# A two-layer Griffin and pooling trunk: another source for four weight units, another order inside a head, another order of seven products, another end

## The chip, the cores and the metric

The kernel runs on one core of one Trainium2 chip. A core has a matrix engine (TensorE, PE), a vector engine (VectorE, DVE), a scalar engine (ScalarE, ACT), a general engine (GpSimd, POOL) and a sync engine (SyncE, SP) that here only starts transfers. The metric is the device time of one call in microseconds (us); the kernel before has a median of 1735.13 us over 3 runs (1734.38 to 1735.78).

## The reference

One sequence of 1024 tokens, width 1024, two layers. Each layer adds a gated token mixer and then a gated squared-ReLU MLP; layer 0 mixes with a Griffin recurrent block, layer 1 with a pooling mixer. Cut to what matters here:

```python
def recurrent_mixer(h, w_y, b_y, w_in, b_in, conv_w, conv_b, w_a, b_a, w_x, b_x, lam, w_out, b_out):
    gate_branch = jax.nn.gelu(h @ w_y + b_y)
    xr = causal_depthwise_conv(h @ w_in + b_in, conv_w, conv_b)      # width 4
    gate_r = sigmoid(block_diag_linear(xr, w_a, b_a))                # 4 heads of 256 channels
    gate_i = sigmoid(block_diag_linear(xr, w_x, b_x))
    log_a = 8 * gate_r * log_sigmoid(lam); a = exp(log_a)
    u = sqrt(-expm1(2 * log_a)) * (gate_i * xr)
    xr = scan(a, u)                                                  # h_t = a_t h_(t-1) + u_t
    return (xr * gate_branch) @ w_out + b_out

for i in range(2):
    x = x + gt_m * mixer_i(modulate(rms_norm(x, g_mix), sh_m, sc_m))
    h = modulate(rms_norm(x, g_ffn), sh_f, sc_f)
    x = x + gt_f * (relu(h @ w1) ** 2 @ w2)                          # 1024 -> 4096 -> 1024
return rms_norm(x, g_final)
```

## The kernel before

Channels lie on the 128 partitions, in 8 blocks of 128; the tokens lie along the free axis, in two halves of 512 (`H`). Half 0 is a tile named `...a` (`xa`, `xca`), half 1 one named `...b`. Every float32 product is made of three matmuls (`mm3`, lines 188 to 190): the operand is split into a high part and a remainder, and high by high, high by remainder and remainder by high are added in one PSUM tile. A projection of one output block over 1024 inputs takes 24 matmuls of 128x512; `acc_mm()` gives the PSUM tiles, six of them in turn, so a product waits until the tile of the sixth product before it has been read.

A weight unit of 128x1024 is loaded and split in two halves of 512 columns. ACT casts the high part (line 180) and DVE subtracts to get the remainder (line 181). In the form `"dma"` (`neg_part`) ACT casts (163) and writes the negated high part (164), and a transfer that POOL starts (165) adds the weight from memory to it; no DVE work is in it.

The stages, in order of time: 0 to 66 us the conditioning, the first norm and the first projections; 66 to 120 us the second half of the input projections `w_in` with the convolutions (line 452 copies a product to `xr`, 459 makes the first of the four taps on ACT, 466 the three others on DVE, or 463 on ACT and 464 on POOL for two of the 16 blocks); up to about 250 us the four heads; then `w_out`, and from 355 us the MLP of layer 0, the pooling mixer and the MLP of layer 1, and the end.

In a head (line 583 on), each half goes through `gates` (the input's split at 534, sigmoids 544, exp and tanh 551 and 552, DVE's product 557, square root 560, scan 564) and then through two `gelu_block`s (572): per half 24 matmuls of gates and 48 of gelu. Sigmoid, exp and tanh, square root and gelu each need their own activation table, so ACT loads four tables per half.

In an MLP round `f2_fast` (line 783 on) makes the second product with seven block products in place of eight, four times (`r` = 0 to 3), six matmuls to a product. What becomes of a product: 1 is copied by ACT and scaled, and POOL adds it to `xb`; 5 and 3 are added by DVE to `xa` (800; 5 twice); 6 is summed by DVE with the copy of 1 (830), scaled by ACT (804) and added by POOL to `xa` (809); 7 is summed on top of that (834), scaled, and added by POOL to both halves; 2 and 4 are added by DVE to `xb`. 3 and 6 go to the same block of `xa`. Their order before is 1, 5, 6, 3, 7, 2, 4.

Each engine works through its own queue in order. The program is written once; a scheduler orders each engine's instructions, with `tc.issue_after` as a bound, and the one DVE instruction that carries the conditioning vector's products (`mb`, line 207) is spread over the heads and rounds as its transfers land ("drip").

At the end the last 256 tokens of half 1 are normed: line 1067 scales blocks 0 and 1 ahead of time into `two`, 1070 copies the broadcast factor for POOL, 1072 multiplies on POOL, 1035 makes blocks 2 to 7 on DVE, and SP starts the four stores (1073, 1037).

## Time and profile before

| what | value |
|---|---|
| median of 3 runs | 1735.13 us (1734.38 to 1735.78) |
| the profiled execution | 1736.2 us, its span 1734.4 us |
| PE busy | 1690.3 us, 97% of the span, 7482 matmuls |
| DVE, ACT, POOL busy | 75%, 58%, 31% |
| mean granted clock of TensorE | 0.994 |

The span runs from the first to the last instruction that the profiler saw; 1.8 us of the execution lie around it. A share of busy time is a mean over stages: here PE is busy nearly always, and the few places where it is not are found by asking what it waited for, and in which stretch.

### The profile page before, as it was taken

The numbers are of one execution on the slowest core, as the hardware profiler recorded it, in microseconds if no ns is written. First come the engines' busy times: TensorE is split into PE (matmuls) and PEld (weight loads), VectorE is DVE, ScalarE is ACT, GpSimd is POOL, SyncE is SP. The second block draws the span as 40 slices with busy tenths as digits, with TensorE's granted clock in tenths as the row PEclk, the third lists the DMA queues.
The fourth block names the chain that finished last, engine by engine and source line by source line (L and its number), as shares of the span: only waits on it lengthen the run. The fifth ranks groups of instructions, "written<-read, shape, count | busy, mean of one in ns | idle before, by whom it ended". The sixth has DMA issues, their size and how long they took to land.

```text
span 1734.4 us, 21031 instructions
## 1 busy us (share of the span) xinstructions
PE 1690.3 (97%) x7482; PEld 1388.3 (80%) x7482; DVE 1308.3 (75%) x2066; ACT 1003.0 (58%) x1717; POOL 538.9 (31%) x471
## 2 busy tenths in 40 slices
PE   6999999999999999999999999999999999999997
PEld 4778778887878888888888888888888888888887
DVE  7896977499898989897973898548586867677646
ACT  5868886565445454545457787756555555555532
POOL 1142343104141405051416233324241516051503
PEclk9999999999999999999999999999999999999998
DMA  9432425552423333342319898872323324150502
GB/s 356 138 104 92 146 86 163 116 153 78 134 82 113 101 94 113 94 124 83 121 43 203 194 195 186 185 163 69 89 79 68 100 52 111 43 121 25 134 1 97
DMA packets 70952, 201.50 MB, mean 116 GB/s; under 512 B 7616, under 2 KB 10048, under 8 KB 70848
## 3 DMA queue, kind: packets, MB, share of 16 engines
q1 hardware_dynamic: 47376, 157.43, 28.2%
q0 software_dynamic: 23472, 42.74, 15.0%
q8 instruction: 58, 0.95, 0.2%
q14 instruction: 46, 0.38, 0.1%
HBM read 195.94 MB, written 4.19 MB: 115 GB/s over the span
## 4 chain that ended last, share of the span: by engine, by line
PE 65%; DVE 19%; issue 6%; ACT 4%; POOL 3%; DMA 2%; DVEq 0%; SPq 0%; ACTq 0%; POOLq 0%
PE mm L188 21%; PE mm L189 21%; PE mm L190 21%; DVE xa L800 2%; POOL xa L809 2%; DVE xb L800 2%; DVE mb L207 1%; DMA mb<-in_wmod 1%; DVE w_a_s L181 1%; DVE raw_w L755 1%; ACT c L804 1%; DVE w_a_a L181 1%; DVE xcb L466 1%; DVE xca L466 1%; PE mm L427 1%
## 5 line engine op out<-in xcount | busy, mean ns | idle before, releaser
L188 PE MATMUL mm<-hh,w_w 128*128 128x512 f32 x1024 | 399.1, 390 | 0.0
L189 PE MATMUL mm<-hl,w_w 128*128 128x512 f32 x1024 | 398.6, 389 | 0.0
L190 PE MATMUL mm<-hh,w_w 128*128 128x512 f32 x1024 | 398.5, 389 | 0.0
L809 POOL TENSOR_TENSOR xb<-xb,c 128x512 f32<-128x512 f32 x104 | 151.2, 1454 | 567.0 <-ACT c L804 566.5
L188 PEld LDWEIGHTS mm<-hh,w_w 128*128 128x128 f32 x1024 | 192.2, 188 | 41.3 <-DVE xa L800 1.6
L190 PEld LDWEIGHTS mm<-hh,w_w 128*128 128x128 f32 x1024 | 192.2, 188 | 39.9
L189 PEld LDWEIGHTS mm<-hl,w_w 128*128 128x128 f32 x1024 | 192.2, 188 | 39.9
L809 POOL TENSOR_TENSOR xa<-xa,c 128x512 f32<-128x512 f32 x104 | 157.0, 1510 | 132.3 <-ACT c L804 132.3
L804 ACT ACTIVATE c<-c,mod 128x512 f32<-128x512 f32 x104 | 75.3, 724 | 175.9 <-DVE c L830 113.5
L165 POOL DMA_DIRECT2D w_w<-in_w x136 | 121.6, 930 | 176.9 <-ACT w_w L164 135.8
L650 ACT ACTIVATE relu<-mm 128x512 f32<-128x512 f32 x128 | 76.2, 595 | 143.0 <-PE mm L190 143.0
L800 DVE SCALAR_TENSOR_TENSOR xa<-mm,mod,xa 128x512 f32<-128x512 f32 x156 | 113.3, 744 | 41.6 <-POOL xa L809 41.6
L207 DVE SCALAR_TENSOR_TENSOR mb<-mb,cond 128x1024 f32<-128x1024 f32 x80 | 114.5, 1434 | 33.2 <-DMA mb<-in_wmod 33.0
L163 ACT CAST w_w<-raw_w 128x512 fp32r<-128x512 f32 x136 | 83.0, 611 | 29.1 <-PE mm L190 29.0
L800 DVE SCALAR_TENSOR_TENSOR xb<-mm,mod,xb 128x512 f32<-128x512 f32 x104 | 77.2, 742 | 19.8 <-POOL xb L809 19.0
L164 ACT ACTIVATE w_w<-w_w 128x512 fp32r<-128x512 f32 x136 | 85.7, 631 | 3.6
L188 PE MATMUL mm<-u,w_a_a 128*128 128x512 f32 x200 | 79.2, 396 | 4.0 <-DVE xa L800 2.3
L640 DVE TENSOR_TENSOR u<-usq,u 128x512 fp32r<-128x512 f32 x102 | 70.3, 689 | 16.1 <-ACT u L639 15.8
L188 PE MATMUL mm<-u,w_w 128*128 128x512 f32 (+1 forms) x224 | 81.0, 362 | 0.0
L189 PE MATMUL mm<-u,w_w 128*128 128x512 f32 (+1 forms) x224 | 80.6, 360 | 0.1
L190 PE MATMUL mm<-u,w_w 128*128 128x512 f32 (+1 forms) x224 | 80.4, 359 | 0.0
L189 PE MATMUL mm<-u,w_a_a 128*128 128x512 f32 x200 | 78.0, 390 | 0.0
(330 smaller groups left out, 4026.1 us busy)
## 6 DMA issues: line engine op xcount, KB each, us to landing
raw_w<-in_w SPq DMA_DIRECT2D x148, 512.0 KB, 4.2
mb<-in_wmod SPq DMA_DIRECT2D x80, 512.0 KB, 3.8
w_w<-in_w POOLq DMA_DIRECT2D x136, 256.0 KB, 5.6
mw<-in_wmod SPq DMA_DIRECT2D x16, 512.0 KB, 9.8
raw_in<-in_w_in SPq DMA_DIRECT2D x8, 512.0 KB, 6.0
raw_y<-in_w_y SPq DMA_DIRECT2D x8, 512.0 KB, 3.7
raw_o<-in_w_out SPq DMA_DIRECT2D x8, 512.0 KB, 4.6
outT<-o SPq DMA_DIRECT2D x11, 256.0 KB, 2.9
```

The source lines that it names most:

```text
L163: S.copy(w[:, 0, 0:n], raw)
L164: S.activation(w[:, 1, 0:n], w[:, 0, 0:n].bitcast(F32), AF.Identity, scale=-1.0)
L165: nc.gpsimd.dma_start(w[:, 1, 0:n], src, accum_op=ALU.add)
L188: PE.matmul(out=ps, lhsT=wh, rhs=rh, start=first, stop=False)
L189: PE.matmul(out=ps, lhsT=wh, rhs=rl, start=False, stop=False)
L190: PE.matmul(out=ps, lhsT=w[:, 1, c:c + P], rhs=rh, start=False, stop=last)
L207: V.scalar_tensor_tensor(raw, raw, 1.0, cond, op0=ALU.mult, op1=ALU.mult, accum_out=m[:, e:e + 1])
L640: eng.tensor_sub(u[n][:, 1, jj, :], src, u[n][:, 0, jj, :].bitcast(F32))
L650: S.activation(r, ps, AF.Relu)
L800: V.scalar_tensor_tensor(xb, ps, g[:, r + 4 * row:r + 4 * row + 1], xb, op0=ALU.mult, op1=ALU.add)
L804: S.activation(t, src, AF.Identity, scale=g[:, r + 4 * row:r + 4 * row + 1])
L809: G.tensor_add(xb, xb, t)
```

## The change

It has four parts.

1. `w_in` units 2, 3, 4 and 5 take the form `"dma"`. Units 2 and 3 are asked for right behind the interleaved product of units 6 and 7, ahead of the convolutions of half 0; 4 and 5 inside the loop, two blocks ahead.
2. `gates` is cut in `split_x`, `sigmoids` and `states`, and `gelu_block` in `gelu_blocks` and `gated`. A head now runs gates of half 0, gelu of half 0, gelu of half 1, gates of half 1; the four gelu activations stand behind the square roots of half 0, in one run. The input split of the gates and the gate weights of the next head are issued a round ahead. `w_out` unit 0 is split on DVE, ahead of the last gates; unit 1 to 3 as before on POOL.
3. The default order of the products of `f2_fast` is 1, 5, 3, 6, 7, 2, 4.
4. At the end `two` is scaled earlier, the output blocks share one tile `olast`, DVE starts with block 2, SP stores blocks 2 to 4 and 0 to 1, and ACT's queue stores 5 to 7.

```diff
@@ -485,6 +485,7 @@
     for k in range(NB):
         for m in (6, 7):
             mm3(ps2[m - 6], uin[m], k * P, hh[1][:, k, :], hl[1][:, k, :], k == 0, k == NB - 1)
+    uin.update({m: split_unit(w_in[m], f"in{m}", "dma") for m in (2, 3)})
     for e in last:
         behind.enter_context(tc.issue_after(e.ins))
     for m in range(3, NB):
@@ -492,8 +493,8 @@
     for m in (6, 7):
         conv(m, conv_input(m, ps2[m - 6], 1), 1)
     for m in range(6):
-        if 0 < m < 5:
-            uin[m + 1] = split_unit(w_in[m + 1], f"in{m + 1}")
+        if m in (1, 2):
+            uin[m + 3] = split_unit(w_in[m + 3], f"in{m + 3}", "dma")
         conv(m, conv_input(m, proj(uin[m], hh[1], hl[1]), 1), 1)
 
 
@@ -526,13 +527,17 @@
 
     behind.close()
 
-    def gates(hd, unit, h):
+    def split_x(hd, h):
 
         xchl = slot("xchl", (2, 2, H), F32R)
         xch, xcl = xchl[:, 0, :, :], xchl[:, 1, :, :]
         src = xc[h][:, 2 * hd:2 * hd + 2, :]
         S.copy(xch, src)
         V.tensor_sub(xcl, src, xch.bitcast(F32))
+        return xch, xcl
+
+    def sigmoids(hd, unit, h, xch, xcl):
+
         rs, gs = [], []
         for mi in range(2):
             b = 2 * hd + mi
@@ -543,6 +548,10 @@
                 t = tmp("gate")
                 S.activation(t, ps, AF.Sigmoid, bias=vcol("ba" if g == 0 else "bx", b))
                 (rs if g == 0 else gs).append(t)
+        return rs, gs
+
+    def states(hd, h, rs, gs):
+
         aa = []
         for mi in range(2):
             b = 2 * hd + mi
@@ -557,7 +566,7 @@
             V.scalar_tensor_tensor(rs[mi], e, 1.0, rs[mi], op0=ALU.add, op1=ALU.mult)
         for mi in range(2):
             b = 2 * hd + mi
-            S.activation(rs[mi], rs[mi], AF.Sqrt)
+            root = S.activation(rs[mi], rs[mi], AF.Sqrt)
             hs = xc[h][:, b, :]
             G.tensor_mul(gs[mi], gs[mi], hs)
             V.tensor_mul(gs[mi], gs[mi], rs[mi])
@@ -565,12 +574,19 @@
                                  op0=ALU.mult, op1=ALU.add)
             if h == 0:
                 V.tensor_copy(carry[:, b:b + 1], hs[:, H - 1:H])
-
-    def gelu_block(m, unit, h):
-        ps = proj(unit, hh[h], hl[h])
-        g = tmp("gelu")
-        S.activation(g, ps, AF.Gelu_apprx_tanh, bias=vcol("by", m))
-        V.tensor_mul(xc[h][:, m, :], xc[h][:, m, :], g)
+        return root
+
+    def gelu_blocks(hd, units, h, g, root):
+        for mi in range(2):
+            ps = proj(units[mi], hh[h], hl[h])
+
+            with tc.issue_after(root.ins):
+                S.activation(g[:, 2 * h + mi, :], ps, AF.Gelu_apprx_tanh, bias=vcol("by", 2 * hd + mi))
+
+    def gated(hd, h, g):
+        for mi in range(2):
+            y = xc[h][:, 2 * hd + mi, :]
+            V.tensor_mul(y, y, g[:, 2 * h + mi, :])
 
     yh, yl = [None, None], [None, None]
 
@@ -580,17 +596,32 @@
             S.copy(yh[h][:, k, :], xc[h][:, k, :])
             V.tensor_sub(yl[h][:, k, :], xc[h][:, k, :], yh[h][:, k, :].bitcast(F32))
 
+
+
+    wo = []
+    ug, xs = split_unit(w_g[0], "g0"), [split_x(0, 0), split_x(0, 1)]
     for hd in range(4):
         rate[0] = hd
-        ug = split_unit(w_g[hd], f"g{hd}")
         uy = [split_unit(w_y[m], f"y{m}") for m in (2 * hd, 2 * hd + 1)]
-        for h in range(2):
-            gates(hd, ug, h)
-            if (hd, h) == (3, 1):
-                split_y(0)
-            for mi in range(2):
-                gelu_block(2 * hd + mi, uy[mi], h)
-    wo = [split_unit(w_out[m], f"o{m}", G, 0) for m in range(4)]
+        first = sigmoids(hd, ug, 0, *xs[0])
+        if hd < 3:
+            xs[0] = split_x(hd + 1, 0)
+        root = states(hd, 0, *first)
+        g = slot("gelu")
+        gelu_blocks(hd, uy, 0, g, root)
+        gated(hd, 0, g)
+        gelu_blocks(hd, uy, 1, g, root)
+        if hd < 3:
+            next_ug = split_unit(w_g[hd + 1], f"g{hd + 1}")
+        else:
+            wo.append(split_unit(w_out[0], "o0", None, 0))
+            split_y(0)
+        second = sigmoids(hd, ug, 1, *xs[1])
+        if hd < 3:
+            ug, xs[1] = next_ug, split_x(hd + 1, 1)
+        states(hd, 1, *second)
+        gated(hd, 1, g)
+    wo += [split_unit(w_out[m], f"o{m}", G, 0) for m in range(1, 4)]
     split_y(1)
 
     af = [None, None]
@@ -780,7 +811,7 @@
         w = neg_part(raw, w2[i, c, r, :, 256:768], "a12_a22")
         return {2: (w, 0, (1, 0)), 4: (w, 256, "t4")}
 
-    def f2_fast(i, c, ahead, products=(1, 5, 6, 3, 7, 2, 4), side=iter(())):
+    def f2_fast(i, c, ahead, products=(1, 5, 3, 6, 7, 2, 4), side=iter(())):
 
 
 
@@ -1056,22 +1087,37 @@
                 G.tensor_mul(o[:, k, 0:n1], o[:, k, 0:n1], bc)
             nc.sync.dma_start(osrc[:, k0:k0 + 4, H:H + n1], o[:, k0:k0 + 4, 0:n1])
         yield
+        for k in range(2):
+            S.activation(two[:, k, :], x[1][:, k, n1:H], AF.Identity, scale=vcol("gfin", k))
+        yield
 
     n1 = 256
+    two = tmp("two").rearrange("p (k t) -> p k t", k=2)
     sa = last_chunk(0, 0, H, "VVVVVVVV")
     sb = last_chunk(1, 0, n1, "VVVVVVVV", once(lambda: final_norm(rstd_bcast(sa), 0, 0, H)))
     sc = last_chunk(1, n1, H - n1, "VVVVVVXX", mid_norm())
-
-    two = tmp("two").rearrange("p (k t) -> p k t", k=2)
-    for k in range(2):
-        S.activation(two[:, k, :], x[1][:, k, n1:H], AF.Identity, scale=vcol("gfin", k))
+    o = slot("olast", (NB, H - n1))
     last_bc = rstd_bcast(sc)
     bc_two = tmp("bc_two", H - n1)
+
+    def last_o(k):
+        V.scalar_tensor_tensor(o[:, k, :], x[1][:, k, n1:H], vcol("gfin", k), last_bc, op0=ALU.mult, op1=ALU.mult)
+
+    def store(eng, k0, k1):
+        eng.dma_start(osrc[:, k0:k1, H + n1:2 * H], o[:, k0:k1, :])
+
+
+    last_o(2)
     S.copy(bc_two, last_bc)
     for k in range(2):
-        G.tensor_mul(two[:, k, :], two[:, k, :], bc_two)
-    nc.sync.dma_start(osrc[:, 0:2, H + n1:2 * H], two)
-    final_norm(last_bc, 1, n1, H - n1, 2)
+        G.tensor_mul(o[:, k, :], two[:, k, :], bc_two)
+    for k in (3, 4):
+        last_o(k)
+    store(nc.sync, 2, 5)
+    store(nc.sync, 0, 2)
+    for k in (5, 6, 7):
+        last_o(k)
+    store(nc.scalar, 5, 8)
 
 
 def _layout(inputs):

```

Where the instructions stand now. First POOL's queue at the input projections; `w_in2` and its like are transfers, `xca` and `xcb` the adds of taps (half 0 and half 1). Before:

```order
L165 DMA w_in0_0_595<-in_w_in 128x512
L165 DMA w_in0_512_599<-in_w_in 128x512
L165 DMA w_in1_0_605<-in_w_in 128x512
L165 DMA w_in1_512_609<-in_w_in 128x512
L464 TENSOR_TENSOR xca_1_470<-xca_1_470,tap_724 128x512
L464 TENSOR_TENSOR xca_1_470<-xca_1_470,tap_727 128x512
L464 TENSOR_TENSOR xca_1_470<-xca_1_470,tap_730 128x512
L464 TENSOR_TENSOR xcb_1_472<-xcb_1_472,tap_748 128x512
L464 TENSOR_TENSOR xcb_1_472<-xcb_1_472,tap_751 128x512
L464 TENSOR_TENSOR xcb_1_472<-xcb_1_472,tap_754 128x512
L562 TENSOR_TENSOR gate_1051<-gate_1051,xca_0_469 128x512
```

After the change:

```order
L165 DMA w_in1_0_605<-in_w_in 128x512
L165 DMA w_in1_512_609<-in_w_in 128x512
L165 DMA w_in2_0_713<-in_w_in 128x512
L165 DMA w_in2_512_717<-in_w_in 128x512
L165 DMA w_in3_0_723<-in_w_in 128x512
L165 DMA w_in3_512_727<-in_w_in 128x512
L464 TENSOR_TENSOR xca_1_470<-xca_1_470,tap_744 128x512
L464 TENSOR_TENSOR xca_1_470<-xca_1_470,tap_747 128x512
L464 TENSOR_TENSOR xca_1_470<-xca_1_470,tap_750 128x512
L165 DMA w_in4_0_811<-in_w_in 128x512
L165 DMA w_in4_512_815<-in_w_in 128x512
L165 DMA w_in5_0_853<-in_w_in 128x512
```

Four transfers stand ahead of the six adds, three between their two groups and one behind them. On PE the three units 2, 3 and 4 were begun in turn with two matmuls each before a remainder was first used; now each unit's 24 matmuls stand together:

```order
L188 MATMUL mm_837<-hh1_0_613,w_in2_0_791 128x512
L189 MATMUL mm_837<-hl1_0_615,w_in2_0_791 128x512
L188 MATMUL mm_877<-hh1_0_613,w_in3_0_831 128x512
L189 MATMUL mm_877<-hl1_0_615,w_in3_0_831 128x512
L188 MATMUL mm_917<-hh1_0_613,w_in4_0_871 128x512
L189 MATMUL mm_917<-hl1_0_615,w_in4_0_871 128x512
L190 MATMUL mm_837<-hh1_0_613,w_in2_0_791 128x512
L188 MATMUL mm_837<-hh1_0_613,w_in2_0_791 128x512
```

```order
L188 MATMUL mm_861<-hh1_0_613,w_in2_0_713 128x512
L189 MATMUL mm_861<-hl1_0_615,w_in2_0_713 128x512
L190 MATMUL mm_861<-hh1_0_613,w_in2_0_713 128x512
L188 MATMUL mm_861<-hh1_0_613,w_in2_0_713 128x512
L189 MATMUL mm_861<-hl1_0_615,w_in2_0_713 128x512
L190 MATMUL mm_861<-hh1_0_613,w_in2_0_713 128x512
L188 MATMUL mm_861<-hh1_0_613,w_in2_0_713 128x512
L189 MATMUL mm_861<-hl1_0_615,w_in2_0_713 128x512
```

So PE reads the remainder of unit 2 (line 190) at its third matmul there, where it stood at the seventh.

ACT in one of the heads (lines 534, 544, 560, 572 before; 535, 549, 569, 584 now). Before, behind the tanh of half 0:

```order
L552 ACTIVATE gate_1602<-gate_1602,ncoef_1005 128x512
L534 CAST xchl_1976<-xcb_1_472 128x1024
L560 ACT_TABLE_LOAD
L560 ACTIVATE gate_1584<-gate_1584 128x512
L560 ACTIVATE gate_1602<-gate_1602 128x512
L572 ACT_TABLE_LOAD
L572 ACTIVATE gelu_1660<-mm_1635,vec_79 128x512
L572 ACTIVATE gelu_1688<-mm_1663,vec_79 128x512
L544 ACT_TABLE_LOAD
L544 ACTIVATE gate_1701<-mm_1694,vec_79 128x512
L544 ACTIVATE gate_1710<-mm_1703,vec_79 128x512
```

After the change, from the table of the square roots of the same half on:

```order
L569 ACT_TABLE_LOAD
L569 ACTIVATE gate_1581<-gate_1581 128x512
L569 ACTIVATE gate_1599<-gate_1599 128x512
L584 ACT_TABLE_LOAD
L584 ACTIVATE gelu_1635<-mm_1636,vec_79 128x512
L584 ACTIVATE gelu_1635<-mm_1662,vec_79 128x512
L584 ACTIVATE gelu_1635<-mm_1690,vec_79 128x512
L180 CAST w_y6_0_1830<-raw_y6_1819 128x512
L180 CAST w_y6_512_1833<-raw_y6_1819 128x512
L180 CAST w_y7_0_1847<-raw_y7_1836 128x512
L584 ACTIVATE gelu_1635<-mm_1716,vec_79 128x512
L180 CAST w_y7_512_1850<-raw_y7_1836 128x512
```

The run of sigmoids that stood behind two gelus now stands behind four; a head has seven table loads where it had eight. The weight casts between are those of `w_y`.

DVE in round 2 of layer 1, behind the last weight split for `r` = 3 (830 and 834 before are 861 and 865 now). Before:

```order
L181 TENSOR_TENSOR w_s_10787<-raw_w_1_2_3_10772,w_s_10787 128x256
L800 SCALAR_TENSOR_TENSOR xa_81<-mm,mod_5_6526,xa_81 128x512
L800 SCALAR_TENSOR_TENSOR xa_82<-mm,mod_5_6526,xa_82 128x512
L830 TENSOR_TENSOR c_10797<-mm,c_10797 128x512
L800 SCALAR_TENSOR_TENSOR xa_81<-mm,mod_5_6526,xa_81 128x512
L834 TENSOR_TENSOR c_10797<-mm,c_10797 128x512
L800 SCALAR_TENSOR_TENSOR xb_83<-mm,mod_5_6526,xb_83 128x512
L800 SCALAR_TENSOR_TENSOR xb_84<-mm,mod_5_6526,xb_84 128x512
L800 SCALAR_TENSOR_TENSOR xa_81<-mm,mod_5_6526,xa_81 128x512
```

After the change:

```order
L181 TENSOR_TENSOR w_s_10783<-raw_w_1_2_3_10768,w_s_10783 128x256
L831 SCALAR_TENSOR_TENSOR xa_81<-mm,mod_5_6439,xa_81 128x512
L831 SCALAR_TENSOR_TENSOR xa_82<-mm,mod_5_6439,xa_82 128x512
L831 SCALAR_TENSOR_TENSOR xa_81<-mm,mod_5_6439,xa_81 128x512
L861 TENSOR_TENSOR c_10793<-mm,c_10793 128x512
L865 TENSOR_TENSOR c_10793<-mm,c_10793 128x512
L831 SCALAR_TENSOR_TENSOR xb_83<-mm,mod_5_6439,xb_83 128x512
L831 SCALAR_TENSOR_TENSOR xb_84<-mm,mod_5_6439,xb_84 128x512
```

The third addition to `xa` (product 3) stood behind the sum `c` of product 6; now it stands directly behind the two of product 5, and the two sums follow each other.


## Rows read from the trace of the kernel before

**Rows 1.** TensorE's waits: what it waited for, us in total, times, longest.

```profile
PE mm L188 <- DVE xa L800: 6.6, 8, 1.6
PE mm L188 <- ACT gelu L572: 5.3, 4, 2.2
...
PE mm L190 <- DVE w_in L181: 3.3, 1, 3.3
```

**Rows 2.** Stretches: length, busy time of PE, PEld, DVE, ACT, POOL, then PEclk.

```profile
66.00:120.00 54.00, 50.73 (x211) 41.34 (x210) 52.72 (x89) 40.55 (x65) 23.30 (x10) 0.94 0.34 89
120.00:250.00 130.00, 124.74 (x533) 101.63 (x532) 103.99 (x145) 107.44 (x144) 43.46 (x29) 0.97 0.37 118
415.00:525.00 110.00, 105.39 (x460) 85.70 (x460) 95.79 (x150) 49.84 (x89) 38.88 (x25) 1.00 0.35 112
525.00:900.00 375.00, 374.11 (x1643) 307.37 (x1642) 320.93 (x510) 183.25 (x324) 105.98 (x67) 1.00 0.32 98
1200.00:1640.00 440.00, 437.12 (x1917) 358.76 (x1916) 305.81 (x453) 240.01 (x419) 159.78 (x138) 1.00 0.34 82
```

**Rows 3.** The same view over two stretches at the lower granted clock.

```profile
97.51:104.33 6.82, 6.00 (x14) 4.75 (x15) 6.82 (x8) 3.03 (x4) 5.22 (x4) 0.50 0.21 64
179.42:182.82 3.40, 3.40 (x9) 2.67 (x9) 3.40 (x8) 3.37 (x6) 0.49 (x1) 0.50 0.00 0
```

**Rows 4.** Timeline of PE: start, us, instruction, idle time before and releaser.

```profile
93.77 0.39 PE L189 MATMUL mm<-hl,w_in 128*128 128x512 f32 x1
...
94.68 0.39 PE L189 MATMUL mm<-hl,w_in 128*128 128x512 f32 x1
98.33 0.79 PE L190 MATMUL mm<-hh,w_in 128*128 128x512 f32 x1 [3.27 <-DVE w_in L181]
```

**Rows 5.** Timeline of DVE in that place.

```profile
80.34 12.68 DVE L466 SCALAR_TENSOR_TENSOR xca<-xr,vec,xca 128x512 f32<-128x512 f32 x19
...
96.53 1.75 DVE L181 TENSOR_TENSOR w_in<-raw_in,w_in 128x512 fp32r<-128x512 f32 x1
```

**Rows 6.** Timeline of POOL from 67 to 103 us.

```profile
72.97 0.86 POOL L165 DMA_DIRECT2D w_in<-in_w_in  x1 [2.65 <-ACT xr L452]
82.76 14.97 POOL L464 TENSOR_TENSOR xca<-xca,tap 128x512 f32<-128x512 f32 x3 [8.93 <-ACT tap L463]
97.69 5.20 POOL L464 TENSOR_TENSOR xcb<-xcb,tap 128x512 f32<-128x512 f32 x3
```

**Rows 7.** The page, DMA issues: count, KB each, median us to landing.

```profile
w_w<-in_w POOLq DMA_DIRECT2D x136, 256.0 KB, 5.6
```

**Rows 8.** Timeline of ACT in two halves of heads: sigmoids, then square roots.

```profile
145.80 2.43 ACT L544 ACTIVATE gate<-mm,vec 128x512 f32<-128x512 f32 x4
...
153.93 1.30 ACT L560 ACTIVATE gate<-gate 128x512 f32<-128x512 f32 x2
...
173.65 0.63 ACT L560 ACTIVATE gate<-gate 128x512 f32<-128x512 f32 x1 [2.45 <-DVE gate L557]
176.46 0.63 ACT L560 ACTIVATE gate<-gate 128x512 f32<-128x512 f32 x1 [2.18 <-DVE gate L557]
```

**Rows 9.** Timeline of PE in a round of layer 1.

```profile
1291.65 0.39 PE L190 MATMUL mm<-ut,w_a_s 128*128 128x512 f32 x1
1292.59 0.50 PE L188 MATMUL mm<-ut,w_s_s 128*128 128x512 f32 x1 [0.56 <-DVE xa L800]
```

**Rows 10.** Timeline of DVE in that round.

```profile
1288.89 0.67 DVE L830 TENSOR_TENSOR c<-mm,c 128x512 f32<-128x512 f32 x1
1291.79 0.75 DVE L800 SCALAR_TENSOR_TENSOR xa<-mm,mod,xa 128x512 f32<-128x512 f32 x1 [2.22 <-POOL xa L809]
```

**Rows 11.** Timeline of POOL in that round.

```profile
1290.46 1.29 POOL L809 TENSOR_TENSOR xa<-xa,c 128x512 f32<-128x512 f32 x1 [3.10 <-ACT c L804]
```

**Rows 12.** Timeline of SP at the end.

```profile
1728.72 0.37 SPq L1073 DMA_DIRECT2D outT<-two  x1
1729.19 1.50 SPq L1037 DMA_DIRECT2D outT<-o  x3
```

## The prediction

> **What bounds the kernel now.** I read the waits of the matrix engine first, since the page has PE busy for 97% of the span: what can be gained is the time in which PE stands or runs slowly, and no other engine's saving counts unless PE waited for it. The list names three causes that the change touches: product tiles waiting for DVE's additions to `xa` (6.6 us, 8 times), the gelu of the heads (5.3 us, 4 times) and one remainder of `w_in` (3.3 us, once) [rows 1]. Then I read the stretches, to see where these lie and what the granted clock does behind them: PE's idle time is the stretch less its busy time, 3.27 us in 66 to 120, 5.26 in 120 to 250, 4.61 in 415 to 525, 0.89 in 525 to 900 and 2.88 in 1200 to 1640 [rows 2]. Last I read the timelines at one wait of each kind. Matmul starts stand 0.23 us apart where nothing waits (93.77 to 94.68 is four of them) [rows 4].
>
> A wait costs more than its idle time in two ways. Behind the 3.27 us the granted clock is 0.50 for 6.82 us, which is 1.2 of 2.4 GHz: PE's 6.00 busy us there would have taken 3.00. Behind a gelu wait it is 0.50 for 3.40 us; there are two such places, 1.70 us lost at each [rows 3]. And even a short wait has a slow start: at 1291.65 the next start comes after 0.94 us, and that matmul takes 0.50 us instead of 0.39, so 0.56 us of idle time cost 0.71 + 0.11 = 0.82 [rows 9].
>
> **The change part by part.** The number of matmuls stays, so the sum is made of stalls only. It is made against the profiled execution, 1736.2 us, which is 1.1 us above the median of the runs.
>
> *The source of `w_in`.* The wait at 98.33 goes through DVE: its remainder subtraction starts at 96.53, behind 19 convolution steps that hold DVE from 80.34 to 93.02 [rows 4, 5]. With a transfer in its place DVE is not asked. Removed: eight subtractions of DVE. Added: eight negations on ACT, whose waits end nothing on PE in this stretch, and eight transfers on POOL at 0.86 us each, landing 5.6 us behind their issue [rows 6, 7]. Units 2 and 3 are issued ahead of POOL's tap adds, which began at 82.76 [rows 6]; ACT has four casts and four negations at 0.61 us (2.43 for four such tiles [rows 8]) to put in front, so I estimate the last issue before 88 and the landings from 86 to 93. They are needed from 94.0 on (the remainder now stands four matmuls earlier than at 98.33, where PE stood from 94.9), one half unit every 2.7 us. So the stall goes: 3.27 + 3.00 = 6.3 us. What is late next: unit 4's two transfers stand behind three tap adds that end at 97.73 (82.76 + 14.97), so they are issued at 97.7 and 98.6 and land at 103.3 and 104.2 [rows 6, 7]; the PE reaches their remainders 48 and 60 matmuls behind 94.0, at 104.9 and 107.6. Unit 5's second half stands behind three more adds of 5.20 us together, issue 105.6, landing 111.2, needed at 113.1. Margins of 1.6 and 1.9 us are less than what one transfer differs from the next, so I put 0.7 us for a late one; between 0 and 6.3 (a stall like the old one).
>
> Here a rule speaks against the change. The first row: three tap adds took 14.97 us under DVE's streak, the next three 5.20 [rows 5, 6]. The Trainium skill ("SBUF — State Buffer", "Who interferes with whom") says that a DVE instruction with two SBUF inputs contends with a GpSimd instruction that reads SBUF; by that rule, the trace agrees. It says further that a transfer which seems stalled by DVE was one that GpSimd has to describe, starved of its port. By that sentence units 2 and 3 would be issued only behind the streak; this is the first rival, worked out below from rows. The issue at 72.97 took 0.86 us, but outside the streak, so it does not settle the matter.
>
> *The heads.* Idle 5.26 us and two slow stretches of 1.70, together 8.7 us [rows 2, 3]. Where nothing waits, the chain from the first sigmoid of a half to the end of its roots takes 9.4 us (145.80 to 155.23); elsewhere two waits for DVE's product, behind conditioning work of DVE that itself waits for transfers, add 2.45 and 2.18 us [rows 8]. Before, a gelu tile was needed again 72 matmuls behind the gates, 16.3 us, and the chain with a table load and the gelu was longer than that. Now a gelu tile of half 0 is needed only for the third product of the next gates: 48 + 48 + 12 = 108 matmuls, 24.5 us. That wait goes even with the 4.6 us. What is late next: the second gates of a head are followed by the next head's gates and gelu of half 0, 72 matmuls or 16.3 us, and then a tile is needed which the next head's first sigmoid reads. This sigmoid stands on ACT behind the chain of the old half: about 12.1 us (the 9.4, a table load and the first sigmoids) undisturbed, 16.7 with both DVE waits. So at three edges between heads 0 to 1.5 us are open; I take 1.0 us in all, and the term is 7.7. At worst each edge stalls by 1.5 us and has a slow stretch of 1.7 behind it, 9.6 in all, and the term is -0.9. The last edge, to `w_out`, has 96 matmuls of cover, 21.8 us, for the chain, five more casts and seven subtractions at about 0.65, some 18 to 22 us by the same rows, while most blocks are needed up to 5 us later; 0.3 us.
>
> *The order of the products.* In a layer 1 round, DVE's addition of product 3 (1291.79) waits 2.22 us for POOL, which adds product 6 to the same block, which waits for ACT, which waits for DVE's sum at 1288.89 [rows 10, 11]. PE waits for that addition, since product 6 of the next `r` takes that tile. With 3 ahead of 6 the addition starts where the sum started, at 1288.89, and the sum ends about 1290.2; its tile is needed at 1291.9, and product 7's, whose sum must wait for ACT's scaling (another 0.8 us behind), at 1293.2 against 1292.0. So the 0.82 us go five times, 4.1 us. In 525 to 900 the wait is for product 4's addition behind the same chain; it comes somewhat earlier, 0.8 of 0.89 idle us with its restarts. In 415 to 525 DVE has weight splits and conditioning in its queue as well and is late by its work alone; I take half the idle time, 2.3. Together 7.2 us, between 3.5 (layer 1 alone, some of it lost to the two sums now side by side) and 11 (all idle time with its restarts).
>
> *The end.* The stores were issued at 1728.72 and from 1729.19 on, the last by 1730.69 [rows 12]. Now they are three instead of four on two queues; DVE makes one block while ACT copies the factor and then waits for that copy. The last issue comes about half a us earlier, the same bytes have to land. 0, between -0.5 and +0.5.
>
> Sum: 6.3 - 0.7 + 7.7 - 0.3 + 7.2 + 0 = 20.2 us. 1736.2 - 20.2 = 1716.0 as a profiled execution, 1714.9 in the frame of the median: **1715 us**.
>
> **The rivals.**
>
> *Transfers starved.* POOL cannot issue units 2 and 3 until the streak ends at 93.0; they land from 99.5 on, 5.5 us late, with a slow clock behind: the `w_in` term is zero or a little below. 1736.2 - 7.4 - 7.2 - 1.1 = 1720 or 1721. For it: the adds at 14.97 us. Against: a transfer's issue reads no tile of SBUF as an add does.
>
> *The edge of the head.* The wait moves from gelu to the next head's sigmoid and costs what it cost: 1736.2 - 5.6 - 7.2 + 0.9 - 1.1 = 1723. For it: ACT's waits for DVE behind conditioning transfers, which the change leaves. Against: 4.6 us of such waits are the most that one half shows in the rows.
>
> *The order of the products does little.* DVE is late by its own work, as in 415 to 525, and only a part of 7.2 comes, say 2: 1720.
>
> *Slower than before.* The three adds ahead of unit 4 are all starved: the queue with four transfers ahead of it starts them later, and DVE's convolutions of half 1 run beside them. If each takes as long as the first three together less two short ones (14.97 - 2 x 1.73 = 11.5), 34.5 us from about 88, unit 4 is issued at 122.5 and lands at 128.1, 23 us late, with 3.0 behind it. Gains of 6.3 + 7.4 + 7.2 = 20.9 against 26: 1740. It decides from a delay of 18 us on. Against: DVE's queue runs out of work that does not wait for these adds, so the starving ends by itself.
>
> **How the numbers follow.** The forecast has 0.60, starved transfers 0.10, the edge of the head 0.10, the product order 0.12, three of these at once (near 1733) 0.03, slower 0.05. The first four are all faster by more than 0.2% (3.5 us, about what a measurement of this kernel can tell from no change), and so are two together, near 1727. So faster 0.92, same 0.03, slower 0.05. The likeliest case alone reaches from 1710 (every stall gone, no new one) to 1719; the range takes in the single rivals and two together, 1707 to 1727.
>
> **What would show it.** In the trace of the changed kernel: no wait of PE for a remainder of `w_in` and a granted clock of 1.00 from 66 to 250 us; POOL's transfers for units 2 and 3 issued before 88 us and landed before 94; in the heads no wait for gelu, and none above 0.5 us for a sigmoid; in layer 1 DVE's third `xa` addition with no wait for POOL, and PE busy for all but 0.2 us of 1200 to 1640. The prediction is wrong if PE stands for unit 4 or 5 of `w_in`, at the third or fourth product tile of a head, or at the first matmuls of `w_out` of half 1.

## The result, and the profile after

The change made the kernel faster, by a little less than half of what was forecast: 1725.54 us (1723.79 to 1726.38, 5 runs) against 1735.13 (1734.38 to 1735.78, 5 runs), ratio 0.9944 [0.993, 0.9959]. That is 9.6 us where 20.2 were forecast. The profiled execution also took 1725.54 us, its span 1723.8 where it was 1734.4.

TensorE's waits in the changed kernel (what it waited for, us in total, times, longest), to be held against [rows 1]:

```profile
PE mm L188 <- ACT gate L549: 5.6, 3, 4.1
...
PE mm L188 <- DVE xa L831: 3.5, 3, 1.3
...
PE mm L188 <- ACT gelu L584: 2.1, 1, 2.1
...
PE mm L189 <- DVE yl L597: 0.4, 1, 0.4
```

The wait for the remainder of `w_in` is gone and the eight for `xa` (6.6 us) are three. The gelu's 5.3 us in four waits became one of 2.1, but a new line stands above all others: 5.6 us for the sigmoids (L549). So the heads stall for 7.7 us where they stalled for 5.3.

The stretches of [rows 2], shifted by what was gained ahead of them, and then those at the lower clock (length, busy time of PE, PEld, DVE, ACT, POOL, PEclk, DMA share, GB/s):

```profile
66.00:120.00 54.00, 54.00 (x239) 44.66 (x238) 52.69 (x84) 48.07 (x79) 25.18 (x18) 1.00 0.61 130
120.00:250.00 130.00, 122.37 (x520) 99.33 (x520) 98.37 (x131) 96.02 (x129) 39.51 (x28) 0.97 0.35 109
410.00:520.00 110.00, 105.59 (x459) 85.53 (x458) 102.10 (x155) 50.40 (x89) 39.76 (x26) 1.00 0.34 110
520.00:895.00 375.00, 375.00 (x1651) 309.36 (x1650) 323.25 (x510) 185.74 (x326) 109.24 (x68) 1.00 0.31 97
1190.00:1630.00 440.00, 440.00 (x1943) 364.50 (x1942) 295.25 (x461) 240.91 (x422) 173.03 (x139) 1.00 0.35 84
181.99:185.40 3.41, 3.41 (x10) 2.66 (x9) 3.41 (x6) 3.39 (x6) 0.00 (x0) 0.50 0.01 2
240.00:243.40 3.40, 3.20 (x8) 2.52 (x9) 3.40 (x4) 3.37 (x6) 2.60 (x2) 0.50 0.01 2
```

PE is busy without a gap in the input stage, in the later rounds of layer 0 and in layer 1. In 120 to 250 it idles 7.63 us, more than the 5.26 before, and it still has two slow stretches of 3.4 us. In 410 to 520 nothing changed: 4.41 idle, 4.61 before.

Measured between the first matmuls of the stages in the two profiled executions, beside the forecast's terms:

| stage | before | after | gain | forecast |
|---|---|---|---|---|
| `w_in` to the gates | 62.2 | 55.9 | +6.3 | +5.6 |
| the heads | 140.2 | 142.9 | -2.7 | +7.7 |
| `w_out` to the MLP | 88.5 | 89.2 | -0.7 | -0.3 |
| rounds 0 and 1 of `f2_fast`, layer 0 | 82.0 | 82.4 | -0.4 | +2.3 |
| rounds 2 to 5 | 154.7 | 152.8 | +1.9 | +0.8 |
| `f2_fast` of layer 1 | 234.4 | 228.5 | +5.9 | +4.1 |
| the end | 60.2 | 60.4 | -0.2 | 0 |

That is 10.1 of the span's 10.6 us; the rest lies in stages that the change doesn't touch. These terms fall 10.1 us short of 20.2: the heads alone account for 10.4 and rounds 0 and 1 for 2.7, while layer 1, rounds 2 to 5 and `w_in` gave 3.6 more than forecast.

**Where the heads' time went.** ACT's timeline in the changed kernel, with the start, the duration and in brackets the idle time and its releaser, from the first sigmoids of one head to those of the next but one:

```profile
164.13 2.42 ACT L549 ACTIVATE gate<-mm,vec 128x512 f32<-128x512 f32 x4
...
176.31 0.63 ACT L569 ACTIVATE gate<-gate 128x512 f32<-128x512 f32 x1 [3.63 <-DVE gate L566]
178.16 0.63 ACT L569 ACTIVATE gate<-gate 128x512 f32<-128x512 f32 x1 [1.21 <-DVE gate L566]
...
202.14 2.42 ACT L549 ACTIVATE gate<-mm,vec 128x512 f32<-128x512 f32 x4
...
221.47 1.84 ACT L549 ACTIVATE gate<-mm,vec 128x512 f32<-128x512 f32 x3
229.02 0.62 ACT L180 CAST w_o<-raw_o 128x512 fp32r<-128x512 f32 x1 [5.70 <-DMA raw_o<-in_w_out]
229.54 0.68 ACT L549 ACTIVATE gate<-mm,vec 128x512 f32<-128x512 f32 x1
...
239.46 2.42 ACT L549 ACTIVATE gate<-mm,vec 128x512 f32<-128x512 f32 x4
```

```profile
164.13:202.14 38.01, 35.17 (x146) 28.05 (x144) 30.12 (x39) 29.83 (x40) 12.43 (x8) 0.96 0.41 127
202.14:239.46 37.32, 33.27 (x144) 26.87 (x144) 29.15 (x37) 28.04 (x38) 10.70 (x8) 1.00 0.35 111
```

ACT takes 38.0 and 37.3 us for a head; PE's 144 matmuls of it take 32.7 at 0.227. ACT's own work (fifth figure of a row) is 29.8 and 28.0 us, and its waits are the rest: four waits for DVE's product, 8.0 us, in the first, and in the second two such of 3.4 and one of 5.70 for a raw block of `w_out`, with the head's last sigmoid queued behind that cast. A head on ACT is one closed chain, both halves in series, since each half's sigmoids stand behind the roots of the half before; beside PE's 32.7 us it leaves 3 to 5 us of room for waits. PE pays at the three edges between heads (164.87, 202.88 and 240.20, waits for a sigmoid) and once inside a head (180.84, for a gelu):

```profile
164.87 0.50 PE L188 MATMUL mm<-hh,w_y 128*128 128x512 f32 x1 [0.46 <-ACT gate L549]
...
180.84 0.50 PE L188 MATMUL mm<-xchl,w_g 128*128 128x512 f32 x1 [2.07 <-ACT gelu L584]
...
202.88 0.50 PE L188 MATMUL mm<-hh,w_y 128*128 128x512 f32 x1 [1.04 <-ACT gate L549]
...
235.76 0.39 PE L190 MATMUL mm<-hh,w_y 128*128 128x512 f32 x1
240.20 0.79 PE L188 MATMUL mm<-hh,w_y 128*128 128x512 f32 x1 [4.05 <-ACT gate L549]
```

The eight matmuls from 240.20 to 243.63 take 3.43 us at the half clock, where eight take 1.81 at the full one.

What DVE's product waited for is in DVE's own queue. Its timeline at an earlier pair of roots, and ACT's:

```profile
150.74 0.68 DVE L181 TENSOR_TENSOR w_g<-raw_g,w_g 128x512 fp32r<-128x512 f32 x1
155.50 1.23 DVE L207 SCALAR_TENSOR_TENSOR mb<-mb,cond 128x1024 f32<-128x1024 f32 x1 [4.08 <-DMA mb<-in_wmod]
...
156.65 1.22 DVE L536 TENSOR_TENSOR xchl<-xcb,xchl 128x1024 fp32r<-128x1024 f32 x1
157.79 0.69 DVE L566 SCALAR_TENSOR_TENSOR gate<-asq,gate 128x512 f32<-128x512 f32 x1
160.31 1.23 DVE L207 SCALAR_TENSOR_TENSOR mb<-mb,cond 128x1024 f32<-128x1024 f32 x1 [1.84 <-DMA mb<-in_wmod]
...
161.47 0.69 DVE L566 SCALAR_TENSOR_TENSOR gate<-asq,gate 128x512 f32<-128x512 f32 x1
```

```profile
158.51 0.63 ACT L569 ACTIVATE gate<-gate 128x512 f32<-128x512 f32 x1 [3.06 <-DVE gate L566]
162.19 0.63 ACT L569 ACTIVATE gate<-gate 128x512 f32<-128x512 f32 x1 [3.05 <-DVE gate L566]
```

DVE stands 4.08 and 1.84 us at a conditioning step (L207) whose data are still on the way, and the product L566 stands behind it. The transfer is late because it is asked for late: the conditioning blocks and the raw weights share one pool of three buffers (`rawp`), and SP can start a load only when a buffer is given back. SP's timeline shows it for the two loads above, the step's and the `w_out` block's:

```profile
150.84 0.33 SPq L222 DMA_DIRECT2D mb<-in_wmod  x1
```

```profile
225.30 3.81 SPq L99 DMA_DIRECT2D raw_o<-in_w_out  x3
```

The first of them is issued when DVE's split of `w_y` (149.04 to 150.81) has freed a buffer, and DVE goes on 4.66 us later; the second is issued when a conditioning step (222.94 to 225.27) has freed its buffer, and ACT's cast follows at 229.02. In 120 to 260 us DVE's waits for these blocks grew from the first to the second of these lines, before and after:

```profile
DVE mb L207 <- DMA mb<-in_wmod: 12.5, 9, 2.2
```

```profile
DVE mb L207 <- DMA mb<-in_wmod: 20.7, 9, 4.1
```

**The input stage.** POOL's timeline in the changed kernel:

```profile
80.66 0.88 POOL L165 DMA_DIRECT2D w_in<-in_w_in  x1 [6.53 <-DVE hl L318]
82.40 0.87 POOL L165 DMA_DIRECT2D w_in<-in_w_in  x1 [0.86 <-PE mm L190]
84.43 0.86 POOL L165 DMA_DIRECT2D w_in<-in_w_in  x1 [1.16 <-ACT w_in L164]
86.36 0.86 POOL L165 DMA_DIRECT2D w_in<-in_w_in  x1 [1.06 <-ACT w_in L164]
87.18 10.71 POOL L464 TENSOR_TENSOR xca<-xca,tap 128x512 f32<-128x512 f32 x3
97.84 2.67 POOL L165 DMA_DIRECT2D w_in<-in_w_in  x3
```

DVE's streak of convolution steps lay from 80.43 to 93.02 here. The four issues inside it took 0.86 to 0.88 us each, as long as the one at 72.97 before [rows 6], and landed 4.9 to 7.3 us behind their issue, at 86.05 to 92.92; the four issued from 66.98 to 73.28 landed 5.8 to 8.7 us behind theirs. The adds behind them took 10.71 for three, against 5.42 for the next three; taken one by one, the first lasted 7.09 us, until the streak was over, and the two others 1.84 and 1.62. So the adds were slow beside the streak and the transfers were not. The Trainium skill ("SBUF — State Buffer", "Who interferes with whom") lets two-input steps of DVE contend with GpSimd's reads, and infers of one such step, `tensor_tensor`, that it leaves the write side free, which describing a transfer needs. The trace agrees with both for the `scalar_tensor_tensor` steps here, by the 10.71 and by the 0.86 us. What the prediction drew from its sentence on starved transfers, issues held back until the streak ends, did not come beside these steps.

**Layer 1.** DVE in a round of the changed kernel, at the place of [rows 10]:

```profile
1278.48 2.06 DVE L831 SCALAR_TENSOR_TENSOR xa<-mm,mod,xa 128x512 f32<-128x512 f32 x3
1280.46 0.68 DVE L861 TENSOR_TENSOR c<-mm,c 128x512 f32<-128x512 f32 x1
1282.04 0.69 DVE L865 TENSOR_TENSOR c<-mm,c 128x512 f32<-128x512 f32 x1 [0.90 <-ACT c L835]
```

The three additions to `xa` run without a gap, and the one wait that is left, 0.90 us for ACT's scaling, reaches nobody: PE has no idle time from 1190 to 1630.

### The profile page after: what moved, and what is told of

Same layout as the page of the kernel before. It is cut to its first block, busy times and chain, and to the rows that moved or that the text cites. A ratio compares the mean times of both kernels' runs of the same rounds, so it can differ in the third digit from the quotient of the medians.

```text
span 1723.8 us, 21072 instructions
## 1 busy us (share of the span) xinstructions
PE 1684.5 (98%) x7482; PEld 1388.2 (81%) x7482; DVE 1299.2 (75%) x2060; ACT 1000.1 (58%) x1720; POOL 552.7 (32%) x477
## 4 chain that ended last, share of the span: by engine, by line
PE 83%; DVE 9%; issue 3%; ACT 2%; DMA 2%; POOL 0%; DVEq 0%; SPq 0%; POOLq 0%; ACTq 0%
PE mm L188 27%; PE mm L189 27%; PE mm L190 27%; DMA mb<-in_wmod 2%; DVE mb L207 1%; PE mm L427 1%; PE sm L294 1%; DVE xa L831 0%; DVE mw L350 0%; DVE xb L831 0%; DVE gate L566 0%; DVE w_y L181 0%; DVE w_w L181 0%; DMA xa<-in_xT 0%; DVE xcb L466 0%
## 5 line engine op out<-in xcount | busy, mean ns | idle before, releaser
L840 POOL TENSOR_TENSOR xb<-xb,c 128x512 f32<-128x512 f32 x104 | 169.4, 1629 | 526.7 <-ACT c L835 526.7
L840 POOL TENSOR_TENSOR xa<-xa,c 128x512 f32<-128x512 f32 x104 | 170.3, 1637 | 137.6 <-ACT c L835 137.6
L165 POOL DMA_DIRECT2D w_w<-in_w x136 | 127.6, 1008 | 182.3 <-ACT w_w L164 146.2
L207 DVE SCALAR_TENSOR_TENSOR mb<-mb,cond 128x1024 f32<-128x1024 f32 x80 | 106.0, 1327 | 50.1 <-DMA mb<-in_wmod 49.9
L831 DVE SCALAR_TENSOR_TENSOR xa<-mm,mod,xa 128x512 f32<-128x512 f32 x156 | 109.3, 741 | 12.1 <-POOL xa L840 12.1
L164 ACT ACTIVATE w_w<-w_w 128x512 fp32r<-128x512 f32 x136 | 84.4, 629 | 2.9
```

The source lines that it names most:

```text
L164: S.activation(w[:, 1, 0:n], w[:, 0, 0:n].bitcast(F32), AF.Identity, scale=-1.0)
L165: nc.gpsimd.dma_start(w[:, 1, 0:n], src, accum_op=ALU.add)
L207: V.scalar_tensor_tensor(raw, raw, 1.0, cond, op0=ALU.mult, op1=ALU.mult, accum_out=m[:, e:e + 1])
L831: V.scalar_tensor_tensor(xb, ps, g[:, r + 4 * row:r + 4 * row + 1], xb, op0=ALU.mult, op1=ALU.add)
L840: G.tensor_add(xb, xb, t)
```

## The experiments

Each was timed beside the kernel before, whose median was 1734.65 us beside the parts alone and 1734.87 to 1736.44 beside the others; the ratios are against that. The stage lengths are from each run's profile, between the same landmarks as above.

**Each part alone.** Four kernels, each the kernel before with one of the four parts of the diff.

> The kernel before with the first part alone: the four w_in units by transfer. Theory (the parts add): the wait for the remainder of w_in and the slow clock behind it go, 6.4 us, so 1728.7 us, with PE busy from 66 to 120 us. Rival (the stall only moves on): the gates wait longer for what DVE and POOL owe them, and less than 3 us remain, 1732 or more.

> The kernel before with the second part alone: the heads' new order, with the early w_out unit. Theory (the second part costs time by itself): its own waits for the gates' sigmoids and for the first gelu outweigh the four gelu waits it removes, 2 to 4 us slower, 1737 to 1739 us. Rival (it gains by itself, and lost only because the first part brings the work of the heads forward): 7 us faster, 1728 us.

> The kernel before with the third part alone: products in the order 1, 5, 3, 6, 7, 2, 4. Theory: 5.2 us in layer 1 and 2.0 in rounds 2 to 5 of layer 0, nothing in its first rounds, where DVE has no time left: 7 us faster, 1728 us. Rival (the waits of the first rounds were the same chain, and something else took them up in the changed kernel): 10 us faster or more, 1725 us.

> The kernel before with the fourth part alone: the end. Theory: one store fewer behind the last block, 0.4 to 0.8 us faster, 1734.5 us. Rival: the landings are bound by the bytes, and nothing can be told from no change.

| part alone | us | ratio | `w_in` | heads | rounds 0, 1 | layer 1 |
|---|---|---|---|---|---|---|
| the source of `w_in` | 1731.01 | 0.9978 [0.9969, 0.9987] | 55.9 | 140.5 | 81.6 | 234.5 |
| the heads | 1735.69 | 1.0004 [0.9995, 1.0013] | 60.7 | 138.4 | 84.4 | 234.5 |
| the products | 1725.55 | 0.994 [0.9928, 0.9952] | 61.0 | 139.4 | 80.1 | 228.5 |
| the end | 1734.68 | 1.0 [0.9991, 1.0008] | 60.8 | 138.9 | 81.2 | 234.5 |

The order of the products alone gives all that the whole change gives, 9.1 us by the medians and 10.4 by the ratio, which is its rival's time. The new order of a head gives nothing, where its theory had a loss and its rival a gain, and the end gives nothing that can be told. The heads alone show the same new waits: DVE 19.1 us for conditioning blocks, ACT 4.7 for `raw_o`, PE 5.3 in two waits for the sigmoids.

The source of `w_in` alone gives 3.6 us (3.8 by the ratio), between its theory and its rival. The stall is gone, but at the first gates PE then waits for the remainder of their input:

```profile
PE mm L189 <- DVE xchl L536: 2.1, 1, 2.1
```

In the whole change, which splits that input earlier, this wait does not stand.

The `w_in` and heads columns also show how far a stage wanders without a change: 62.2 and 140.2 in the profile of before, 60.8 and 138.9 with the new end alone. For `w_in` the reason can be read: in all four profiles with the old source that are told of here PE waits 3.2 or 3.3 us for the remainder, but behind that wait the granted clock is 0.50 for 3.4 us in the kernels with the new heads, products or end alone, and for 6.82 us in the profile of before [rows 3]. What makes the difference is not shown.

**The first and third part together, with the old head.**

> The kernel before with the first and the third part, without the heads' new order and without the end. Theory (the second part is what takes the gains back): 3.8 + 10.4 us faster than before as measured one by one, 1720 to 1721 us, that is 4 to 5 us faster than all four parts together. Rival (the gains of the first and third part overlap): 1724 us or more.

Measured 1720.85 us (1719.41 to 1721.76), ratio 0.9916 [0.9902, 0.9929]: the 3.8 and 10.4 us of the two add up, as the theory had it, and without the new head and end the kernel is 4.7 us faster than with them. The heads take 140.3 us instead of 142.9, rounds 0 and 1 80.3 instead of 82.4. In these heads PE waits no less, 6.1 us for gelus and 2.1 for the input's remainder against 7.7 us in the whole change; but the waits are short ones, and the granted clock over the heads is 1.00, where the whole change has 0.98 with its two stretches at 0.50.

**Is it the early block of `w_out`?** Its split goes back behind the heads in the program:

```diff
-            wo.append(split_unit(w_out[0], "o0", None, 0))
...
-    wo += [split_unit(w_out[m], f"o{m}", G, 0) for m in range(1, 4)]
+    wo += [split_unit(w_out[m], f"o{m}", G, 0) for m in range(4)]
```

> The changed kernel with the w_out unit 0 back behind the heads (split on POOL with the others). Theory (the early unit's load stands behind conditioning loads in a ring of three buffers, ACT waits 5.7 us for it with the fourth sigmoid of the last gates but one queued behind, and so the last edge between heads costs 4.05 us and a slow clock): that wait goes, the heads take 137 us instead of 142.9, and the time is 1719 to 1720 us. Rival (the edge is bound by the chain through DVE anyway): the heads take 141 us or more, 1724 us.

Measured 1724.74 us, 0.994 [0.9927, 0.9954], the heads 144.9 us: no better, and its rival's time. ACT still waits 6.6 us for the block, since the scheduler puts the cast in the same place. So the edit did not remove the wait that it was made to remove. That the block is asked for early in the program is not the reason for the wait; what the wait costs, this run leaves open.

**Is it the conditioning steps?** The new head also takes fewer of them: the gate weights of the next head are split under the old head's `rate`, so 15 steps fall into the heads and not 18. One kernel takes 8 (`rate[0] = min(hd, 1)`), one 18 again (`split_unit(w_g[hd + 1], f"g{hd + 1}", None, hd + 1)`).

> The changed kernel with fewer conditioning steps in the heads (at most one to a weight unit, 8 of the 15 stay). Theory (DVE stands 20.7 us for conditioning transfers, and ACT's square roots behind it): that wait falls under 9 us, the waits for sigmoid and gelu at the first two edges and the first gelu (3.6 us and a slow clock) go, the heads take 139 us or less; what is moved out costs 2 to 4 us in the first rounds of the MLP. Time 1723 to 1727 us. Rival (DVE's wait is filled by other waits in the chain, for POOL's square or ACT's tanh): the heads stay at 142 us.

> The changed kernel with the three conditioning steps per gate unit that the second part lost (the next head's gate unit is split while the rate is still that of the head before; 15 steps in the heads instead of 18). Theory: the three steps are what makes the first MLP round of layer 0 take 43.2 us where the third part alone has 40.4; with them back it is 40 to 41 us, the heads take 1 to 3 us more, time 1724 to 1727 us. Rival (the round is long for another reason): it stays at 43 us, and the time rises to 1727 or more.

With 8 steps the heads take 131.5 us; their 576 matmuls alone take 130.6. ACT's head is down to 35.9 and 30.9 us, no wait for `raw_o` is left, and of PE's only 0.6 us for a sigmoid. So it was the conditioning steps that held the heads. By which way is not shown. The theory named DVE's waits for the blocks and had them fall under 9 us, but they are still long:

```profile
DVE mb L207 <- DMA mb<-in_wmod: 15.8, 5, 4.2
```

There are five of them where there were nine, ACT's waits for DVE's product fell from 18.9 to 13.0 us, and the wait for `raw_o` went altogether; no run parts the one from the other. And the time is 1725.68 us, 0.9943 [0.993, 0.9955], as before the edit, since the steps were paid for in another place than the theory had it, the `w_out` stage and not the first rounds: the steps that were put off must be done before the MLP's norm, stand there in a row, and PE waits behind them for the sum of squares, in one piece:

```profile
PE sm L294 <- DVE ssq L264: 7.5, 1, 7.5
```

The `w_out` stage grows from 89.2 to 100.7 us. With 18 steps the first round of `f2_fast` falls from 43.2 to 40.5 us and the heads rise from 142.9 to 145.0: 1724.49, 0.9937 [0.9924, 0.9949], about the same sum. As its theory had it, the lost steps explain the round that became slower, not the heads.

**Can the steps go into the `w_out` stage?** Five kernels looked for a place: one step per unit in every head (`rate[0] = 1`) and two behind each of the first eight `w_out` products (`drip(2)`), with the new head (first) and the old head (third); the same with only 8 steps in the heads (second); and the last two with `min(hd, 1)` in the heads and two steps behind the four later products of half 0 (`elif h == 0: drip(2)`), with the new head and the old.

> The changed kernel with one conditioning step per weight unit in the heads (11 in place of 15) and two instead of one behind each of the first eight w_out products (16 in place of 8). Theory (the heads' chain is held by conditioning steps that wait for their transfers; in the w_out stage DVE and the transfers have room): heads 131 to 134 us, w_out stage 89 to 90, the first MLP round 40 to 41, time 1711 to 1714 us. Rival (the w_out stage cannot take eight steps more: its transfers are at 0.9 of the engines there): that stage takes 95 us or more, and the time is 1719 us or more.

> The changed kernel with 8 conditioning steps in the heads, as in the run with few of them, and two instead of one behind each of the first eight w_out products. Theory: heads 131.5 us as there, w_out stage 89 to 91 instead of 100.7, the first MLP round 43, since three steps fewer than now stand ahead of it; time 1712 to 1716 us. Rival: the 11 us of that w_out stage come from the number of steps in it, not from their standing in one row at its end, and stay: 1724 us.

> First and third part on the old order of the heads, with one conditioning step per weight unit there (12 in place of 18) and two behind each of the first eight w_out products. Theory 1 (the new order of the heads has its own worth, once the conditioning is out of the way: the old one needs a gelu tile again after 16.3 us): heads 136 us or more, 1716 us or more, slower than the same edit on the changed kernel by 3 us. Theory 2 (only the conditioning held the heads, in either order): heads 131 to 133 us, and the time is the same as of that kernel, within 1 us.

> The changed kernel with at most one conditioning step per weight unit in the heads (8), one behind each of the first eight w_out products as before, and two behind each of the next four, where none stood. Theory (the heads are held by the steps, the w_out stage by eight of them standing in one row ahead of the MLP's norm): heads 131 to 133 us, w_out stage 89 to 92, first MLP round 43, time 1713 to 1716 us. Rival (the ring of three load buffers has no room for eight more loads in the w_out stage, wherever they stand): w_out stage 98 us or more, 1722 us or more.

> The same distribution of conditioning steps (9 in the heads) on the first and third part with the old order of the heads. Theory 1 (the new order has its own worth): heads 135 us or more, while the new order takes 131 to 133. Theory 2 (only the steps held the heads): 131 to 133 us as well.

| kernel | us | ratio | heads | `w_out` stage |
|---|---|---|---|---|
| first, new head | 1730.62 | 0.9966 [0.9954, 0.9979] | 136.7 | 103.1 |
| second, new head, 8 steps | 1732.93 | 0.9983 [0.9974, 0.9992] | 134.4 | 105.3 |
| third, old head | 1729.26 | 0.9961 [0.9948, 0.9973] | 139.6 | 98.6 |
| fourth, new head, later steps | 1724.24 | 0.9937 [0.9925, 0.995] | 133.0 | 97.9 |
| fifth, old head, later steps | 1721.48 | 0.9923 [0.9909, 0.9936] | 136.2 | 91.9 |

The first three lose more in `w_out` than the heads gain; for the first this is what its rival had, for the second it is worse than its rival. In the first kernel PE's waits from 120 to 400 us include these two, both in the `w_out` stage:

```profile
PE mm L190 <- DMA w_o<-in_w_out: 6.9, 1, 6.9
PE mm L188 <- ACT w_o L163: 5.3, 1, 5.3
```

They fit a reading by which conditioning blocks among the first products hold the three buffers that the later `w_out` units want; no run tested it by itself. Set behind these products, the steps cost 8.7 us in the `w_out` stage with the new head and give about that back in the heads; the sum stays, close to what that kernel's rival had. No place among these beats the old head with the steps left alone (1720.85 us).

The two pairs also show what the new order of a head is worth once few steps are left in it: the heads are about 3 us shorter than in the old order (136.7 against 139.6, 133.0 against 136.2), as the fifth kernel's first theory had it. It is lost again in the `w_out` stage, which is 4.5 and 6.0 us longer with the new head, so that the new head makes neither kernel the faster one (1730.62 against 1729.26, 1724.24 against 1721.48), where the third one's first theory had it 3 us ahead. Three us are not much beside the spread: the same heads with 8 steps took 131.5, 134.4 and 133.0 us.

**An even spread and an early input split, with the old head.** From the kernel with the first and third part, the old head, 18 steps as 0, 6, 6, 6 where they were 0, 3, 6, 9, and the input of half 0 split ahead of the `w_y` units:

```diff
-        rate[0] = hd
+        rate[0] = min(2 * hd, 2)
...
+        x0 = split_x(hd, 0)
...
-            gates(hd, ug, h)
+            gates(hd, ug, h, *(split_x(hd, 1) if h else x0))
```

> First and third part on the old order of the heads; the 18 conditioning steps spread as 0, 6, 6, 6 over the heads in place of 0, 3, 6, 9, and the gates' input split of half 0 issued ahead of the two w_y units. Theory (crowded steps make the gelu waits, the late input split the wait at the first gates of 2.1 us): the wait at the first gates goes, the gelu waits fall from 6.1 to 3 us, heads 136 us instead of 140.3, time 1716 to 1718 us. Rival (it is the number of steps, wherever they stand): gelu waits of 5 to 7 us, heads 138 us or more, 1719 us or more.

Measured 1717.66 us (1717.09 to 1718.28), ratio 0.99 [0.9883, 0.9916], the fastest of all and faster than the kernels before and after the change. DVE's waits for conditioning blocks in the heads are the shortest of the kernels with 18 steps (10.6 us in eight waits with the two parts alone), and PE's are left at two:

```profile
DVE mb L207 <- DMA mb<-in_wmod: 7.2, 6, 2.4
```

```profile
PE mm L188 <- ACT gelu L577: 5.1, 2, 3.5
```

PE's wait of 2.1 us for the input's split, which the two-part kernel has at its first gates, is gone; the heads take 138.1 us instead of 140.3. The time is the theory's, but the gelu waits (5.1 us, where it had 3) and the heads are the rival's. Of the 3.2 us by which this kernel is ahead of the two-part one, 2.2 lie in the heads and 0.7 ahead of `w_in`, where the two are the same; their intervals overlap, and they were not timed beside each other. How much of the heads' gain is the spread and how much the early split was not taken apart.

## Why the prediction was wrong

*The source of `w_in`* was right in mechanism, and in size nearly: 6.3 us by the two profiles, where 6.3 less 0.7 were forecast. A part of that is luck. The slow clock was priced at 3.00 us from one profile; in three others that keep the old source it lasted half as long, and the stage took 60.7 to 61.0 us, which is 4.9 to 5.1 more than with the new source. The transfers were issued from 80.66 to 86.36, before the 88 that was named, and landed by 92.92, before 94. No late one stalled PE, and the clock stayed at 1.00 to 120 us, though not to the 250 that was named. Starved transfers, the first rival, and tap adds slow enough to make the kernel slower than before are refuted by POOL's rows.

*The heads* are the step that failed, by 10.4 us. The forecast said that the gelu wait "goes even with the 4.6 us" and took 1.0 us for three edges. Two things were wrong in it. It reckoned each half's chain from its own gates and gave it 16.3 or 24.5 us of cover. But the sigmoids of half 0 stand on ACT behind all of the old head, so what comes late at one edge is still late at the next tile: at 180.84, at the third product tile of the second gates, the gelu wait that should have gone is there, 2.07 us, behind an edge that was 0.46 late and 4.84 us of waits at the roots. The sum that decides is ACT's for a whole head, 28 to 30 us of work against 32.7 of PE, which leaves room for 3 to 5 us of waits; there were 8.0 and 9.1. And it took DVE's waits as they stood before, 2.45 and 2.18 us [rows 8]; they grew to as much as 3.63, and a wait for `raw_o` of 5.70 joined them, of which the forecast had nothing. The reckoning of the tiles itself was sound: with most of the conditioning steps out of the way the same order took 131.5 to 134.4 us, and the forecast amounts to 132.5 (140.2 less 7.7).

The rival that was named, the edge of the head, is what happened, and its 1723 was nearer than the forecast. Its price was too low, -0.9 for the heads where -2.7 came, and it had three like stalls where one edge took 4.05 us with 1.6 behind it and the two others 0.46 and 1.04.

*The order of the products* was right in mechanism and too small in size where the chain was read. Layer 1 gave 5.9 us and not 4.1. The forecast priced one late start in a round, 0.82 us, but a round had two. The other stands at 1289.02 in the kernel before, where the weight load waits for additions of DVE to `xa` too; the matmul comes 0.42 us behind the one ahead of it, not 0.23, and PE has next to no idle time there:

```profile
1288.60 0.39 PE L190 MATMUL mm<-ut,w_a_s 128*128 128x512 f32 x1
...
1289.02 0.19 PEld L188 LDWEIGHTS mm<-u,w_a_a 128*128 128x128 f32 x1 [0.46 <-DVE xa L800]
1289.02 0.50 PE L188 MATMUL mm<-u,w_a_a 128*128 128x512 f32 x1
```

The rows of the stretches say the same: 1943 matmuls in 440 us where there were 1917, and 26 at 0.227 us are 5.9. In rounds 2 to 5 it was 1.9 for 0.8, and 1651 matmuls against 1643. Rounds 0 and 1 are the second miss: 2.3 forecast, -0.4 found. Alone the order gained 1.1 to 1.9 there (80.1 against 81.2 and 82.0, the kernels with the new end alone and before); in the whole change the three steps that the heads no longer take fell into the first of them (43.2 us, and 40.5 with the steps put back). The forecast had overlooked that the gate weights' split changed its `rate`.

*`w_out`'s edge* (0.37 us of a wait, 0.7 us by the stage, 0.3 forecast) *and the end* (no difference) were right.

What stays open: why the new head costs more beside the new `w_in` (142.9 us) than alone (138.4), where the old head differs less (140.3 and 140.5 beside it, 138.9 to 140.2 without); why DVE's waits for conditioning blocks grew in the new order although fewer steps fall into it; which of DVE's waits and the wait for `raw_o` costs what; and whether a fourth raw buffer would free the heads, which was not tried.

## What to carry to other kernels

When a loop is pipelined over two engines, add up one whole turn of it (here a head) on the engine that is *not* the bound, its waits included, and compare that with the turn of the one that is; the cover of a single wait says little when lateness is handed on. In an in-order queue, a filler (here a conditioning step) whose data come through a shared pool of buffers is not free: it holds what stands behind it until its own load has landed, and that load starts only when some other user lets a buffer go. A reordering also moves whatever is counted along the program, so count the fillers per stage before and after.

## What the runs showed of the hardware

Four matters were not expected. DMA issues on POOL took 0.86 to 0.88 us in the middle of a DVE streak that stretched three tap adds to 10.71 us. Idle time tells too little of what short waits cost: those for `xa` in layer 1, 2.88 us of idle time in 440, were worth 5.9 us when they went. The same wait of 3.2 or 3.3 us for a remainder was followed by 3.4 us at a granted clock of 0.50 in three profiles and by 6.82 in a fourth. And moving the order of seven products, which adds and removes nothing, was worth 9 to 10 us in a kernel whose matrix engine was already busy for 97% of the time.
